# A score matmul of 64 rows takes 128, with zeros beside the keys' low parts

## The chip, the cores and the metric

The kernel runs on one core of one Trainium2 chip. The metric is the device time of one launch in microseconds. Of the core's engines five matter: PE multiplies matrices (its loads of weights are shown as PEld), DVE does elementwise work and reductions, ACT applies functions and copies, POOL does some elementwise work, and SP issues most transfers. They run side by side, each in its own program order, and wait for each other by semaphores.

## The reference, cut to what matters

One layer of a decoder trunk: 1024 tokens of 1024 channels, everything in float32. A combined projection feeds four mixers, one of which is a differential attention; gates, an output projection, a SwiGLU network and a gated embedding follow. The attention, with the other parts left out:

```python
q = q.reshape(b, s, ATT_HEADS, ATT_V_DIM)          # 4 heads of 128 = 2 x 64
k = k.reshape(b, s, ATT_HEADS, ATT_V_DIM)
k1, k2 = k[..., :ATT_QK_DIM], k[..., ATT_QK_DIM:]
...
def softmax_map(qh, kh):
    sc = jnp.einsum("bqhd,bkhd->bhqk", qh, kh).astype(jnp.float32) * scale + bias
    sc = jnp.where(causal, sc, NEG_LOGIT)
    return jax.nn.softmax(sc, axis=-1)

probs = softmax_map(qblk[..., :ATT_QK_DIM], k1) - lam * softmax_map(qblk[..., ATT_QK_DIM:], k2)
return jnp.einsum("bhqk,bkhd->bqhd", probs.astype(v.dtype), v)
```

Each head has two score maps, each over 64 channels of queries and keys. Queries are taken in blocks of 128; a block sees the keys up to its own end.

## The kernel before, in words

To keep float32 accuracy, each operand of a matmul is split into a high part (rounded to float32r) and a low part (what is missing). A product is then three matmuls: high by high, low by high, high by low (`mm3`, lines 160 to 166). The high part is an ACT copy, the low part a DVE subtraction, or for some weights a POOL subtraction (`split`, lines 72 to 74).

The program starts with the norm of x, its transposes, the values of two heads and the queries and keys of head 0. From about 100 us it runs the attention (`attention`, line 395): four heads of eight query blocks in one stream. Per block PE computes the scores of the *next* block (`scores`), transposes the probabilities of this one (`turn`), does a piece of other projections that no head depends on (the `fills`: the queries and keys of the following head, the values of heads 2 and 3, and in the last head the projections of the conformer branch, whose convolution taps run on DVE), and multiplies by the values (`weigh`). Between a block's scores and its transposes lie, on DVE and ACT, the bias, the row maximum, the exponential of each map and the difference of the two maps.

A score map has 64 channels, half of PE's 128 rows. The queries of a map are therefore held as high parts above low parts (`qs[m]`, 128 rows), and the keys' high parts twice (`kh[m]`, 128 rows), so that one matmul of 128 rows gives high by high plus low by high (line 303). The third product, high queries by low keys, is a matmul over the map's own 64 rows (line 304): the low parts of both maps share one tile `kl[0]`, map 0 in rows 0 to 63 and map 1 in rows 64 to 127, and the queries' high parts lie in the same rows. Map 1 has the halves swapped for that. Both matmuls add into one score tile in PSUM. A score tile is at most 512 columns wide per matmul, so a block of up to 512 keys has two such pairs (one per map), a wider one four.

Each engine runs what is written in program order, as far as its data allow. The tiles `qs`, `kh`, `kl` come from a pool `up` of 38 buffers of 4 KB per partition (line 46), which the later stages use as well. The low parts of the weights of the `fills` are computed on POOL (`eng=nc.gpsimd`, line 771), in order of their use.

After the attention come gates and branch projections, the other mixers, the output projection, the SwiGLU network and the gated embedding, all of them long runs of `mm3`.

Of the kernel before, what the change touches and what calls it, by code (L numbers as in the profile page):

```python
# [11 lines left out]
F32 = mybir.dt.float32  # L12
# [26 lines left out]
def tile_hybrid_layer(ctx: ExitStack, tc: tile.TileContext, a):  # L39
# [35 lines left out]

# [1 line left out]
    ident = cpool.tile([P, P], F32, name="ident")  # L77
# [24 lines left out]
    class HalfT:  # L102
        """A channel-major activation [1024 channels, 1024 tokens] as hi and lo parts."""

# [14 lines left out]
    def transpose_in(pool, tag, src, dst, t):  # L119
        """Eight 128-blocks of src [tokens of tile t, 1024] into dst, split."""  # L120
        h, c0 = t // 4, (t % 4) * P
        for b in range(2):
            ps = pool.tile([P, HF], F32, tag=tag, name=nm("tr"))
            for j in range(4):
                k = 4 * b + j
                nc.tensor.transpose(ps[:, j * P:(j + 1) * P], src[:, k * P:(k + 1) * P], ident)
            v = ps.rearrange("p (g j c) -> p g j c", g=2, j=2)
            for g in range(2):
                hi = dst.hi[h][2 * b + g][:, :, c0:c0 + P]
                lo = dst.lo[h][2 * b + g][:, :, c0:c0 + P]  # L130
                split(hi, lo, v[:, g])

    def load_w(src, nk=NK, eng=None):
        """A column tile [nk * 128, 128] of a weight as hi and lo."""
        raw = wp.tile([P, NK, P], F32, tag="raw", name=nm("raw"), bufs=RAW_BUFS)
        nc.sync.dma_start(raw[:, :nk, :], src.rearrange("(k p) c -> p k c", p=P))
        hi = wp.tile([P, NK, P], F32R, tag="whi", name=nm("whi"))
        lo = wp.tile([P, NK, P], F32R, tag="wlo", name=nm("wlo"))
        split(hi[:, :nk, :], lo[:, :nk, :], raw[:, :nk, :], eng)
        return hi, lo  # L140

    def load_row_w(src, shape, eng=None):
        """As load_row, in the slots of the column tiles."""
        raw = wp.tile(shape, F32, tag="raw", name=nm("raw"), bufs=RAW_BUFS)
        nc.sync.dma_start(raw, src)
        hi = wp.tile(shape, F32R, tag="whi", name=nm("whi"))
        lo = wp.tile(shape, F32R, tag="wlo", name=nm("wlo"))
        split(hi, lo, raw, eng)
        return hi, lo

    def load_row(src, shape, eng=None):
        """Rows of a weight as moving operands: hi and lo in slots of their own."""
        raw = wp.tile(shape, F32, tag="raw", name=nm("raw"), bufs=RAW_BUFS)
        nc.sync.dma_start(raw, src)
        hi = utile(shape, F32R, "rwh")
        lo = utile(shape, F32R, "rwl")
        split(hi, lo, raw, eng)
        return hi, lo

    def mm3(ps, triples, start=True, stop=True):  # L160
        """Sum of exact products of split operands: hi*hi + hi*lo + lo*hi."""
        n = len(triples)
        for i, (lh, ll, rh, rl) in enumerate(triples):
            nc.tensor.matmul(ps, lhsT=lh, rhs=rh, start=start and i == 0, stop=False)  # L164
            nc.tensor.matmul(ps, lhsT=lh, rhs=rl, start=False, stop=False)  # L165
            nc.tensor.matmul(ps, lhsT=ll, rhs=rh, start=False, stop=stop and i == n - 1)  # L166
# [15 lines left out]

# [1 line left out]
    ed = dram.tile([S, D], F32, name="ed")  # L184
# [37 lines left out]
    def load_v(b, load, eng=None):  # L222
        """The value columns of heads 2b and 2b+1, as moving operands."""
        c = C_V + b * 256
        return [load(w_in[q * 512:(q + 1) * 512, c:c + 256].rearrange("(k p) c -> p k c", p=P), [P, 4, 256], eng)
                for q in range(2)]

    def proj_v(b, t, wv):
        """Values of token tile t, per head the hi part beside the lo part."""
        if t % 2 == 0:  # L230
            v_hl[b, t // 2] = utile([P, 2, 2, 2, P], F32R, "vhl")
        ps = mmtile("pv")
        mm3(ps[:, 0:256], [(hT.his(k, t * P, P), hT.los(k, t * P, P), wv[k // 4][0][:, k % 4, :],
                            wv[k // 4][1][:, k % 4, :]) for k in range(NK)])
        v = v_hl[b, t // 2][:, t % 2]
        split(v[:, :, 0, :], v[:, :, 1, :], ps[:, 0:256].rearrange("p (h c) -> p h c", c=P))

    def proj(col, evac, eng=None):
        """Columns col..col+127 of the input projection, channel-major, to evac(half, psum): two steps."""
        w = []  # L240

        ps = {}

        def step(h, part):
            if not w:
                w.extend(load_w(w_in[:, col:col + P], eng=eng))
            hi, lo = w
            if part == 0:
                ps[h] = mmtile("pz")
            ks = range(part * 4, part * 4 + 4)  # L250
            mm3(ps[h], [(hi[:, k, :], lo[:, k, :], hT.his(k, h * HF, HF), hT.los(k, h * HF, HF)) for k in ks],
                part == 0, part == 1)
            if part == 1:
                evac(h, ps[h])

        return [lambda h=h, part=part: step(h, part) for h in range(2) for part in range(2)]

# [1 line left out]
    def proj_qk(h, eng=None):  # L259
        """Of both score maps: queries as hi above lo, keys as hi above hi, and the keys' lo parts; the  # L260
        products over 128 rows are then hi*hi + lo*hi in one pass. Map 1 has the halves swapped."""
        qs, kh, kl = [None] * 2, [None] * 2, [None]
        own = (slice(0, 64), slice(64, P))
# [10 lines left out]
        def evac_k(half, ps):  # L274
            s = slice(half * HF, (half + 1) * HF)
            for m in range(2):
                if half == 0:
                    kh[m] = utile([P, S], F32R, "kh")
                    if m == 1:
                        kl[0] = utile([P, S], F32R, "kl")  # L280
            for m in range(2):
                r, o = own[m], own[1 - m]
                nc.scalar.activation(kh[m][r, s], ps[r], AF.Copy)
                nc.scalar.activation(kh[m][o, s], ps[r], AF.Copy)
                nc.vector.tensor_sub(kl[0][r, s], ps[r], kh[m][r, s].bitcast(F32))

        return (qs, kh, kl), proj(C_Q + h * P, evac_q, eng) + proj(C_K + h * P, evac_k, eng)

    def head(h, qk):
        """One head: its steps per query block and the step that ends it."""  # L290
        q_st, k_hi, k_lo = qk
# [4 lines left out]
        def scores(i):  # L296
# [4 lines left out]
            def score(ps, m, c0, c1):  # L301
                r = slice(m * 64, (m + 1) * 64)
                nc.tensor.matmul(ps, lhsT=q_st[m][:, qs], rhs=k_hi[m][:, c0:c1], start=True, stop=False)
                nc.tensor.matmul(ps, lhsT=q_st[m][r, qs], rhs=k_lo[0][r, c0:c1], start=False, stop=True)

# [89 lines left out]
    def attention(qk, fills):  # L395
        """All heads as one stream of query blocks; the steps of `fills`, which a head does not depend on, lie
        between its blocks."""
        heads, y, ended = {}, [], 0
# [21 lines left out]

# [1 line left out]
    merged = [None] * NK  # L422
# [31 lines left out]

# [1 line left out]
    def conv(c, src, name, bias, j, K, t0, n, ops=None):  # L456
        """c = causal depthwise convolution of src, for tokens t0..t0+n-1 of channel tile j, as single steps."""
        def tap(k):
# [69 lines left out]

# [1 line left out]
    def lru():  # L530
# [58 lines left out]

# [1 line left out]
    def sconv(ys):  # L591
# [57 lines left out]

# [1 line left out]
    hT = HalfT("hT")  # L651
# [22 lines left out]

    # relative-position bias of the two key blocks next to a query block, times 8, less the far bucket's
    tdf = stile(4, "tdf")
# [16 lines left out]

    # per-channel vectors, channels on partitions
    vecs = [("lru_conv_w", 4), ("lru_conv_b", 1), ("lru_ba", 1), ("lru_bx", 1), ("lru_lambda", 1),
# [27 lines left out]

    # lambda of the differential attention, negated, on every partition
    lv = t2tile("lv")
# [10 lines left out]

    # 8 * softplus(-lru_lambda) = 8 * (max(z, 0) + log1p(exp(-|z|))), log1p(e) = 2 atanh(e / (2 + e))
    lam4 = cvec[:, :, pos["lru_lambda"]]
# [28 lines left out]

# [1 line left out]
    fills = []  # L769
# [51 lines left out]

# [1 line left out]
    wo = [load_row(a["w_o"][0][k * P:(k + 1) * P, :], [P, D]) for k in range(NK)]  # L823
# [31 lines left out]

# [1 line left out]
    acc = [None] * NT  # L857
# [68 lines left out]

# [1 line left out]
    out = a["out"][0]  # L928
# [39 lines left out]
def bucket_hot():  # L968
    """Column j is the one-hot T5 bucket of distance 255 - j; zero where the distance is negative."""
    n = 255 - np.arange(384)  # L970
# [24 lines left out]
```

## Time and profile before

| | |
|---|---|
| median of 3 timed runs | 2092.32 us (2092.0 to 2092.96) |
| span of the profiled execution | 2090.1 us |
| PE busy | 2058.9 us (99%), 9405 matmuls |
| DVE busy | 1045.2 us (50%) |
| ACT busy | 696.4 us (33%) |
| POOL busy | 46.5 us (2%), 25 instructions |
| chain that ended last | PE 90%, DVE 5%, DMA 3%, ACT 2% |

The profiled execution's own time, its span, is 2.2 us under the median; the page gives no other time for it. In the profile an engine counts as busy from an instruction's start to its end. PE works on several matmuls at once, one behind the other, so the rows of matmuls that follow each other overlap, and the distance between two starts tells more than a duration. A row of a timeline has the start, the duration, the engine, the line, the operation, what it writes and reads by the program's names, and the shape; "64*128" of a matmul are the rows and columns of its weights, "64x512" the shape of what streams past them. A bracket at a row's end is the time that the engine idled before it, and what it waited for.

### The profile page before, as it was taken

The numbers are of one execution on the slowest core, as the hardware profiler recorded it, in microseconds if no ns is written. First come the engines' busy times: TensorE is split into PE (matmuls) and PEld (weight loads), VectorE is DVE, ScalarE is ACT, GpSimd is POOL, SyncE is SP. The second block draws the span as 40 slices with busy tenths as digits, with TensorE's granted clock in tenths as the row PEclk, the third lists the DMA queues.
The fourth block names the chain that finished last, engine by engine and source line by source line (L and its number), as shares of the span: only waits on it lengthen the run. The fifth ranks groups of instructions, "written<-read, shape, count | busy, mean of one in ns | idle before, by whom it ended". The sixth has DMA issues, their size and how long they took to land.

```text
span 2090.1 us, 22768 instructions
## 1 busy us (share of the span) xinstructions
PE 2058.9 (99%) x9405; PEld 1685.8 (81%) x9405; DVE 1045.2 (50%) x1507; ACT 696.4 (33%) x1167; POOL 46.5 (2%) x25
## 2 busy tenths in 40 slices
PE   7999999999999999999999999999999999999999
PEld 6867877888887888878888788888888888888787
DVE  4476669697957323464333544233434333343574
ACT  5455555422115212563222433321111211112374
POOL 1000111000000000000000000000000000000000
PEclk9999999999999999999999999999999999999999
DMA  7210110011210112112111521211202212022342
GB/s 239 74 31 21 31 31 28 23 46 46 61 51 26 56 50 58 44 31 65 46 51 46 161 101 61 61 61 41 60 21 61 61 41 61 21 61 61 101 136 96
DMA packets 155974, 126.55 MB, mean 61 GB/s; under 512 B 5616, under 2 KB 140721, under 8 KB 155870
## 3 DMA queue, kind: packets, MB, share of 16 engines
q1 hardware_dynamic: 150688, 116.93, 18.2%
q10 hardware_dynamic: 5182, 8.16, 1.1%
q8 instruction: 74, 1.21, 0.2%
q14 instruction: 30, 0.25, 0.0%
HBM read 111.70 MB, written 13.37 MB: 60 GB/s over the span
## 4 chain that ended last, share of the span: by engine, by line
PE 90%; DVE 5%; DMA 3%; ACT 2%; issue 1%; ACTq 0%; DVEq 0%; SPq 0%
PE pz L164 5%; PE pz L165 5%; PE pz L166 5%; PE pg L166 5%; PE pg L165 5%; PE pg L164 5%; PE fu L165 4%; PE fu L166 4%; PE fg L165 4%; PE fg L166 4%; PE fu L164 4%; PE fg L164 4%; PE fo L166 4%; PE fo L164 4%; PE fo L165 4%; PE pb L166 3%
## 5 line engine op out<-in xcount | busy, mean ns | idle before, releaser
L74 DVE TENSOR_TENSOR wlo<-raw,whi 128x1024 fp32r<-128x1024 f32 (+1 forms) x130 | 141.8, 1091 | 339.5 <-ACT whi L73 339.3
L73 ACT ACTIVATE whi<-raw 128x1024 fp32r<-128x1024 f32 (+1 forms) x148 | 143.4, 969 | 462.3 <-PE pg L165 123.4
L164 PE MATMUL pz<-hTh,whi 128*128 128x512 f32 x576 | 229.5, 398 | 2.0 <-ACT scc L600 1.7
L166 PE MATMUL pz<-hTh,wlo 128*128 128x512 f32 x576 | 227.2, 394 | 0.0
L165 PE MATMUL pz<-hTl,whi 128*128 128x512 f32 x576 | 227.1, 394 | 0.0
L166 PE MATMUL pg<-hTh,wlo 128*128 128x512 f32 x512 | 199.1, 389 | 0.5 <-DVE wlo L74 0.5
L165 PE MATMUL pg<-hTl,whi 128*128 128x512 f32 x512 | 199.3, 389 | 0.0
L164 PE MATMUL pg<-hTh,whi 128*128 128x512 f32 x512 | 199.2, 389 | 0.0
L464 DVE SCALAR_TENSOR_TENSOR cfc<-cfu,cvec,cfc 128x994 f32<-128x994 f32 (+14 forms) x120 | 160.4, 1337 | 2.6
L875 DVE TENSOR_TENSOR fsilu<-fu,fsilu 128x512 f32<-128x512 f32 x44 | 30.4, 692 | 259.5 <-PE fu L166 259.5
L893 DVE TENSOR_TENSOR acc<-acc,fo 128x512 f32<-128x512 f32 x160 | 108.9, 686 | 80.8 <-PE fo L166 79.5
L164 PE MATMUL fo<-rwh,fh 128*128 128x512 f32 x352 | 137.5, 390 | 0.2
L165 PE MATMUL fo<-rwl,fh 128*128 128x512 f32 x352 | 137.2, 390 | 0.0
L166 PE MATMUL fu<-h2Th,wlo 128*128 128x512 f32 x352 | 137.0, 389 | 0.0
L166 PE MATMUL fo<-rwh,fl 128*128 128x512 f32 x352 | 137.0, 389 | 0.0
L165 PE MATMUL fu<-h2Tl,whi 128*128 128x512 f32 x352 | 136.9, 389 | 0.0
L164 PE MATMUL fu<-h2Th,whi 128*128 128x512 f32 x352 | 136.9, 389 | 0.0
L164 PE MATMUL fg<-h2Th,whi 128*128 128x512 f32 x352 | 136.9, 389 | 0.0
L165 PE MATMUL fg<-h2Tl,whi 128*128 128x512 f32 x352 | 136.9, 389 | 0.0
L166 PE MATMUL fg<-h2Th,wlo 128*128 128x512 f32 x352 | 136.9, 389 | 0.0
L164 PEld LDWEIGHTS pz<-hTh,whi 128*128 128x128 f32 x576 | 109.0, 189 | 26.9 <-issue 2.8
L166 PEld LDWEIGHTS pz<-hTh,wlo 128*128 128x128 f32 x576 | 108.7, 189 | 24.0 <-issue 1.9
(265 smaller groups left out, 3809.8 us busy)
## 6 DMA issues: line engine op xcount, KB each, us to landing
raw<-in_w_in_dram SPq DMA_DIRECT2D x72, 512.0 KB, 3.8
raw<-in_w_ffn_in_dram SPq DMA_DIRECT2D x44, 512.0 KB, 4.1
raw<-in_w_ffn_out_dram SPq DMA_DIRECT2D x22, 512.0 KB, 3.5
raw<-in_w_branch_dram SPq DMA_DIRECT2D x32, 256.0 KB, 2.7
xt<-in_x_dram SPq DMA_DIRECT2D x8, 512.0 KB, 5.4
ed<-e ACTq DMA_DIRECT2D x16, 256.0 KB, 2.7
xres<-in_x_dram SPq DMA_DIRECT2D x8, 512.0 KB, 4.1
raw<-in_w_o_dram SPq DMA_DIRECT2D x8, 512.0 KB, 5.3
```

The lines of the kernel that those rows point to most:

```text
L73: nc.scalar.activation(dst_hi, src, AF.Copy)
L74: (eng or nc.vector).tensor_sub(dst_lo, src, dst_hi.bitcast(F32))
L164: nc.tensor.matmul(ps, lhsT=lh, rhs=rh, start=start and i == 0, stop=False)
L165: nc.tensor.matmul(ps, lhsT=lh, rhs=rl, start=False, stop=False)
L166: nc.tensor.matmul(ps, lhsT=ll, rhs=rh, start=False, stop=stop and i == n - 1)
L464: nc.vector.scalar_tensor_tensor(o, in0=src[:, a0 - sh:t0 + n - sh], scalar=cv(name, j, k), in1=o, op0=ALU.mult, op1=ALU.add)
L875: nc.vector.tensor_mul(g, pu, g)
L893: nc.vector.tensor_add(acc[t][:, cs], acc[t][:, cs], ps)
```

## The change

The keys' low parts get a tile per map, `kl[0]` and `kl[1]`. Each holds the low parts in the map's own 64 rows, and zeros in the other 64, which POOL writes once per head. Line 304 then multiplies all 128 rows: the queries' low parts meet the zeros.

```diff
-        qs, kh, kl = [None] * 2, [None] * 2, [None]
+        qs, kh, kl = [None] * 2, [None] * 2, [None] * 2
...
                     kh[m] = utile([P, S], F32R, "kh")
-                    if m == 1:
-                        kl[0] = utile([P, S], F32R, "kl")
+                    kl[m] = utile([P, S], F32R, "kl")
+                    nc.gpsimd.memset(kl[m][own[1 - m], :].bitcast(F32), 0.0)
...
-                nc.vector.tensor_sub(kl[0][r, s], ps[r], kh[m][r, s].bitcast(F32))
+                nc.vector.tensor_sub(kl[m][r, s], ps[r], kh[m][r, s].bitcast(F32))
...
             def score(ps, m, c0, c1):
-                r = slice(m * 64, (m + 1) * 64)
                 nc.tensor.matmul(ps, lhsT=q_st[m][:, qs], rhs=k_hi[m][:, c0:c1], start=True, stop=False)
-                nc.tensor.matmul(ps, lhsT=q_st[m][r, qs], rhs=k_lo[0][r, c0:c1], start=False, stop=True)
+                nc.tensor.matmul(ps, lhsT=q_st[m][:, qs], rhs=k_lo[m][:, c0:c1], start=False, stop=True)
```

The rest of the diff drops comments. On PE, DVE, ACT and SP the same instructions stand in the same order; names carry other numbers. On PE these are the scores of the first two blocks of head 0, two maps each (`sc` is the score tile, `kh` and `kl` the keys' parts, `qs` the queries). Before:

```order
L303 MATMUL sc_1029<-kh_726,qs_689 128x128
L304 MATMUL sc_1029<-kl_728,qs_689 128x128
L303 MATMUL sc_1029<-kh_727,qs_692 128x128
L304 MATMUL sc_1029<-kl_728,qs_692 128x128
L303 MATMUL sc_1048<-kh_726,qs_689 128x256
L304 MATMUL sc_1048<-kl_728,qs_689 128x256
```

And now:

```order
L303 MATMUL sc_1032<-kh_726,qs_689 128x128
L304 MATMUL sc_1032<-kl_727,qs_689 128x128
L303 MATMUL sc_1032<-kh_729,qs_692 128x128
L304 MATMUL sc_1032<-kl_730,qs_692 128x128
L303 MATMUL sc_1051<-kh_726,qs_689 128x256
L304 MATMUL sc_1051<-kl_727,qs_689 128x256
```

Nothing moved; the second map reads a low tile of its own. On POOL the memsets come in. From the low parts of the embedding's weights (`wlo_110`) to those of head 1's queries and keys and of the next weights, before:

```order
L74 TENSOR_TENSOR wlo_110<-raw_107,whi_109 128x1024
L74 TENSOR_TENSOR wlo_1075<-raw_1072,whi_1074 128x1024
L74 TENSOR_TENSOR wlo_1315<-raw_1312,whi_1314 128x1024
L74 TENSOR_TENSOR wlo_1611<-raw_1608,whi_1610 128x1024
L74 TENSOR_TENSOR wlo_1770<-raw_1767,whi_1769 128x1024
```

And now:

```order
L74 TENSOR_TENSOR wlo_110<-raw_107,whi_109 128x1024
L281 MEMSET kl_727 64x1024
L281 MEMSET kl_730 64x1024
L74 TENSOR_TENSOR wlo_1078<-raw_1075,whi_1077 128x1024
L74 TENSOR_TENSOR wlo_1318<-raw_1315,whi_1317 128x1024
L281 MEMSET kl_1406 64x1024
L281 MEMSET kl_1409 64x1024
L74 TENSOR_TENSOR wlo_1617<-raw_1614,whi_1616 128x1024
L74 TENSOR_TENSOR wlo_1776<-raw_1773,whi_1775 128x1024
```

A pair of memsets per head stands in front of a subtraction. The same further on, at the two halves of the value weights of heads 2 and 3 and the weights that follow; before:

```order
L74 TENSOR_TENSOR wlo_1889<-raw_1886,whi_1888 128x1024
L74 TENSOR_TENSOR wlo_1895<-raw_1892,whi_1894 128x1024
L74 TENSOR_TENSOR wlo_2402<-raw_2399,whi_2401 128x1024
L74 TENSOR_TENSOR wlo_2561<-raw_2558,whi_2560 128x1024
L74 TENSOR_TENSOR wlo_2680<-raw_2677,whi_2679 128x1024
```

And now:

```order
L74 TENSOR_TENSOR wlo_1898<-raw_1895,whi_1897 128x1024
L281 MEMSET kl_1805 64x1024
L281 MEMSET kl_1808 64x1024
L74 TENSOR_TENSOR wlo_1904<-raw_1901,whi_1903 128x1024
L74 TENSOR_TENSOR wlo_2411<-raw_2408,whi_2410 128x1024
L74 TENSOR_TENSOR wlo_2570<-raw_2567,whi_2569 128x1024
L281 MEMSET kl_2599 64x1024
L281 MEMSET kl_2602 64x1024
L74 TENSOR_TENSOR wlo_2692<-raw_2689,whi_2691 128x1024
```

Head 2's pair stands between the two halves of the value weights, head 3's behind the second weights of the projections that follow.

## Rows read from the trace of the kernel before

**Rows 1.** Windows: busy us (and count) of PE, PEld, DVE, ACT, POOL; clock, DMA.

```profile
173.30:245.00 71.70, 70.20 (x428) 58.10 (x428) 46.56 (x97) 38.34 (x92) 9.50 (x4) 1.00 0.10 30
245.00:307.00 62.00, 62.00 (x292) 47.59 (x290) 35.62 (x74) 36.99 (x74) 7.69 (x4) 1.00 0.09 26
307.00:402.00 95.00, 93.12 (x430) 72.71 (x429) 82.26 (x124) 47.09 (x97) 13.40 (x5) 0.96 0.11 31
307.00:350.00 43.00, 41.12 (x184) 32.14 (x182) 38.94 (x59) 20.86 (x48) 7.06 (x3) 0.92 0.11 31
```

**Rows 2.** Timeline of PE in an input projection of head 2: start us, duration us.

```profile
300.07 0.40 PE L165 MATMUL pz<-hTl,whi 128*128 128x512 f32 x1
300.30 0.40 PE L166 MATMUL pz<-hTh,wlo 128*128 128x512 f32 x1
```

**Rows 3.** Timeline of PE in scores of head 0 and of head 1.

```profile
100.86 0.33 PE L303 MATMUL sc<-kh,qs 128*128 128x128 f32 x1
101.11 0.32 PE L304 MATMUL sc<-kl,qs 64*128 64x128 f32 x1
101.37 0.38 PE L303 MATMUL sc<-kh,qs 128*128 128x256 f32 x1
101.68 0.38 PE L304 MATMUL sc<-kl,qs 64*128 64x256 f32 x1
102.00 0.38 PE L303 MATMUL sc<-kh,qs 128*128 128x256 f32 x1
...
208.90 0.49 PE L303 MATMUL sc<-kh,qs 128*128 128x512 f32 x1
209.32 0.50 PE L304 MATMUL sc<-kl,qs 64*128 64x512 f32 x1
209.75 0.33 PE L352 MATMUL ptr<-ident,prob 128*128 128x128 f32 x1
```

**Rows 4.** Source line 304: durations min/median/max in ns, first and last start, forms.

```profile
L304 PE MATMUL sc<-kl,qs x96: 322/490/580, 100.6 to 389.1; 64*128 64x512 f32 x48, 64*128 64x128 f32 x16, 64*128 64x256 f32 x16, 64*128 64x384 f32 x16
```

**Rows 5.** Timeline of PE: 128-row neighbours of 128 and of 256 columns.

```profile
180.99 1.06 PE L389 MATMUL otr<-ident,oall 128*128 128x128 f32 x8 [1.50 <-DVE mx L324]
181.81 0.48 PE L165 MATMUL pz<-hTl,whi 128*128 128x512 f32 x1
...
216.22 0.28 PE L363 MATMUL av<-vhl,pth 128*128 128x256 f32 x1
216.34 0.28 PE L364 MATMUL av<-vhl,ptl 128*128 128x256 f32 x1
```

**Rows 6.** Timeline of PE's weight loads in the projection of rows 2.

```profile
299.84 0.19 PEld L165 LDWEIGHTS pz<-hTl,whi 128*128 128x128 f32 x1
```

**Rows 7.** Timeline of POOL, PE and DVE: results and the matmuls that read them.

```profile
194.73 2.39 POOL L74 TENSOR_TENSOR wlo<-raw,whi 128x1024 fp32r<-128x1024 f32 x1 [17.22 <-ACT whi L73]
197.18 0.39 PE L165 MATMUL pv<-wlo,hTh 128*128 128x256 f32 x1
...
215.10 1.14 DVE L342 SCALAR_TENSOR_TENSOR prob<-prob,ratio,prob 128x896 f32<-128x896 f32 x1
220.97 0.98 PE L352 MATMUL ptr<-ident,prob 128*128 128x128 f32 x7
```

**Rows 8.** Timeline of PE and DVE: where PE waits in head 0 and head 3.

```profile
110.64 0.44 PE L303 MATMUL sc<-kh,qs 128*128 128x384 f32 x1 [0.24 <-ACT prob L312]
122.32 0.44 PE L352 MATMUL ptr<-ident,prob 128*128 128x128 f32 x1 [1.96 <-DVE prob L342]
307.10 3.23 DVE L464 SCALAR_TENSOR_TENSOR cfc<-cfu,cvec,cfc 128x994 f32<-128x994 f32 x1
310.57 1.11 PE L352 MATMUL ptr<-ident,prob 128*128 128x128 f32 x4 [1.58 <-DVE oall L369]
```

**Rows 9.** Groups of instructions on POOL: busy us, mean ns, idle before.

```profile
L532 POOL MEMSET bd<- 128x1024 f32 x1 | 1.0, 960 | 424.8 <-PE pb L166 424.8
```

**Rows 10.** Windows, columns as in rows 1.

```profile
310.00:315.00 5.00, 4.43 (x12) 3.47 (x13) 5.00 (x11) 2.29 (x8) 0.00 (x0) 0.50 0.36 107
```

## The prediction, made before the changed kernel was run

> **What bounds the kernel now.** I first read the windows view of the attention, the stage in which the change lies [rows 1]. In each stretch PE is the busy engine (70.2 of 71.7 us, 62.0 of 62.0, 93.1 of 95.0), and DVE comes near it only in the last head (82.3 of 95.0). But a PE that counts as busy need not be streaming: a matmul's row lasts until its result is out, so I read starts, not durations. In the timeline of an input projection, 512-column matmuls over 128 rows, each with new weights, start 0.23 us apart [rows 2]. In the timeline of the scores the same width is far slower: line 303 (128 rows) at 208.90, line 304 (64 rows) at 209.32, the next 128-row instruction at 209.75 [rows 3]. That is 0.42 and 0.43 us, about the whole duration of one matmul: wherever the row count changes, the next one starts only when the one before is through. Line 303 has the full shape and is hit as hard as line 304, so it isn't the small matmul that is slow, but the step from 128 to 64 rows and the step back. It happens at every width: 0.25 and 0.26 us at 128 columns (100.86, 101.11, 101.37), 0.31 and 0.32 us at 256 (101.37, 101.68, 102.00) [rows 3].
>
> **The change part by part.** *The second matmul takes 128 rows.* All neighbours then have one shape, and the starts should fall to what 128-row neighbours show: 0.23 us at 512 columns [rows 2], 0.12 at 256 (216.22 to 216.34), and about 0.10 at 128 (eight transposes of 128 columns between 180.99 and 181.81) [rows 5]. For a pair of lines 303 and 304 that saves 0.85 - 0.46 = 0.39 us at 512 columns, 0.63 - 0.24 = 0.39 at 256 and 0.51 - 0.21 = 0.30 at 128. 384 columns lie between two widths that save 0.39, and I take that. The source view counts 48 pairs of 512 columns and 16 each of 384, 256 and 128 [rows 4]: 80 x 0.39 + 16 x 0.30 = 36.0 us, or 9.0 per head. The bound above is that sum, since line 304 can't be cheaper than the neighbours that it comes to equal. The bound below is no gain at all, if the gap belonged to something else in the pair (that both matmuls carry the same queries as weights and add into one bank). Lines 164 to 166 add into one bank as well, with 0.23 us between starts [rows 2], so I take the upper end.
>
> A rule of the skill speaks against this. The Trainium skill, "TensorE: Matmul & The Clock Gate", section "Part 3: Packing small matmuls", says that a weight load overlaps a running matmul only when the row groups differ; with full rows everywhere each load would stand behind the matmul before it. The trace disagrees: with 128 rows on both sides the load of line 165 runs at 299.84 for 0.19 us, and the matmuls around it stay 0.23 us apart [rows 2, 6].
>
> *What comes back as waits.* PE's order is the same before and after, so each saved piece brings PE earlier to results of DVE, ACT and POOL. In most blocks there is room: the probabilities that DVE finishes at 216.24 (215.10 + 1.14) are transposed at 220.97, 4.7 us later, and a block of eight matmuls takes out at most 4 x 0.39 = 1.6 us [rows 7]. There is none in three places:
> - The first four blocks of head 0. The scores of blocks 0 and 1 are issued early, and the third block at 110.64 already waits for an exponential; what blocks 0 and 1 save (2 x 0.30 + 2 x 0.39 = 1.4 us) returns whole. At 122.32 PE has waited 1.96 us for probabilities [rows 8], so of the 1.6 us of blocks 2 and 3 I let 1.3 return, as only their own scores shorten that chain. Together 2.7 us.
> - Head 3, where DVE works off the convolution's taps between the softmax steps. PE waits 1.58 us there at 310.57, behind a tap of 3.23 us [rows 8]. DVE's highest share in a stretch is 38.94 / 43.0 = 0.91 [rows 1]. If it can't pass that, the 95.0 us shrink to 82.26 / 0.91 = 90.8, so 4.2 of the 9.0 us stay and 4.8 return.
> - Edges in heads 1 and 2 where PE starts right behind a result that the scores don't bring forward: POOL's low parts end at 197.12 (194.73 + 2.39) and line 165 starts at 197.18 [rows 7]; the end of a head has PE waiting 1.50 us at 180.99 [rows 5]. About 1 us at each of three such edges, an estimate from these rows, 3.1 us in all.
>
> That returns 10.6 us, and 36.0 - 10.6 = 25.4 stay.
>
> *Eight memsets on POOL.* Each head clears half of two tiles. The only memset of 1024 columns in the trace takes 0.96 us [rows 9], so a pair is 1.9 us and all are 7.7. POOL is the least busy engine (13.4 of 95.0 us at most [rows 1]), and the pairs run when the subtraction before them is done, long before the scores that read them. In front of the next subtraction POOL has idled 17.22 us at 194.73 [rows 7], which covers a pair; if that cover went, a pair would cost up to 1.9 us at one edge. What they may cost beside that is DVE's time, where the two engines hold each other up. Bounds: nothing, or all 7.7 us. I take nothing, since POOL's busy time is far from the length of any stretch and the first pair, by its place in POOL's order, falls well before the attention; the pair between the two halves of the value weights lies nearest to a wait of PE for DVE (180.99 [rows 5]). Here the Trainium skill, "SBUF - State Buffer", section "Who interferes with whom", says that a DVE instruction with two SBUF inputs contends with a GpSimd instruction that reads SBUF, not with one that only writes; by it the price is nothing too, and no run here shows it yet.
>
> *One more 4 KB tile per head* from the 38-buffer pool. It could make later tiles wait. In the built program PE, ACT, DVE and SP wait for the same instructions as before, apart from three waits of DVE for memsets that are long done by then. So nothing.
>
> *The clock.* It is at 1.2 instead of 2.4 GHz in stretches such as 310 to 315 us (mean 0.50), after PE had idled 1.58 us [rows 8, 10]. A longer wait there may lengthen that, by 1 or 2 us, and a removed one may save as much. I count zero and keep it in the range.
>
> The sum: the profiled execution spans 2090.1 us, the timed runs have 2092.3, so some 2.2 us lie around the span and stay. 2090.1 - 25.4 = 2064.7, and 2092.3 - 25.4 = **2067 us** for the timed runs.
>
> **The rivals.**
> 1. *All of it is kept* (2092.3 - 36 = 2056 us): the chains follow PE. For it, the 4.7 us of room in the middle of a head; against it, the waits that stand in rows 8 before anything is saved. A gain over 32 us counts here.
> 2. *The softmax chain takes most.* If heads 1 and 2 keep no more than head 3 (4.2 us each) and head 0 loses its 2.7 us on top: 4 x 4.2 - 2.7 = 14 us, 2078 us. Against it, DVE is busy only 46.6 of 71.7 and 35.6 of 62.0 us there [rows 1]. A gain between 6 and 18 us counts here.
> 3. *The gap stays*, since each weight load (0.19 us [rows 6]) has to follow the matmul before it: a pair of 512 columns then takes 2 x (0.19 + 0.23) = 0.84 us instead of 0.85, and the time stays at about 2092 us. This is the rule cited above. Against it, rows 2 and 6. The change would then not do what it says.
> 4. *Slower: POOL.* Each pair of memsets stands in front of a subtraction on whose result the next projection's matmuls wait, and may hold DVE as well. Up to 25.4 / 4 = 6.3 us per pair that only eats the gain; beyond it the kernel is slower. With 8 us per pair, 2092.3 - 25.4 + 32 = 2099 us. Against it, a pair is 1.9 us long, a third of what it would take.
>
> **How the numbers follow.** Forecast (gain 18 to 32 us) 0.68; rival 1 0.14; rival 2 0.13; rival 3 0.03; rival 4 0.02. The likeliest case alone spans 2060 to 2074. The range goes to the whole 36 us below (2056, with one more for the clock) and to rival 2 above with some 3 us for clock and memsets: 2055 to 2081. A measurement here can tell 0.2%, 4.2 us, from no change. Faster: 0.68 + 0.14 + 0.13 = 0.95; same 0.03; slower 0.02.
>
> **What would show it.** The starts of lines 303 and 304 (304 in the new numbering too) 0.23 us apart at 512 columns and 0.12 at 256: step one right; 0.4 as before: wrong, and rival 3 holds. PE's waits in the attention growing by about 11 us, most of it at the start of head 0 and in head 3, behind DVE and ACT (now 1.96 and 1.58 us at the two largest places [rows 8]): step two right; if they grow by less than 4 us, rival 1; by more than 18, rival 2. The new MEMSET rows on POOL, with a DVE instruction beside them that takes its usual time: the memsets' price of nothing right. The work that now ends at 402 us should end near 377, and all behind it only shift. I am wrong in kind if a wait appears behind the attention, or if a low clock fills more of the attention than before.

## The result, and the profile after

The changed kernel takes 2065.72 us (median of 4 runs, 2062.73 to 2067.35) against 2092.64 us of the kernel before beside it, 26.9 us less. The ratio on record is 0.9863 [0.9848, 0.9879]; it is not the quotient of these two medians (0.9871), and of 2092.64 us it would be 28.7 us (25.3 to 31.8). The forecast was 2067. The profiled execution spans 2062.6 us, 27.5 less than before.

The difference lies almost wholly in the attention. Set side by side, PE's starts stand 0.4 us later than before when the attention begins and 26.9 us earlier from 375 us on (402 before), so the attention is 27.3 us shorter. They stay there until 1966 us (1993 before), where 0.6 us more come from a shorter wait for ACT (0.2 us in place of 0.8). In the windows view PE is busy 1672.73 us behind the attention, and was 1672.63.

PE in the scores of one block of head 1, timeline of the kernel before (start us, duration us, engine, line); this run of scores is longer than that of [rows 3]:

```profile
217.54 0.28 PE L364 MATMUL av<-vhl,ptl 128*128 128x256 f32 x1
217.66 0.39 PE L303 MATMUL sc<-kh,qs 128*128 128x512 f32 x1
217.98 0.49 PE L304 MATMUL sc<-kl,qs 64*128 64x512 f32 x1
218.40 0.50 PE L303 MATMUL sc<-kh,qs 128*128 128x512 f32 x1
218.83 0.50 PE L304 MATMUL sc<-kl,qs 64*128 64x512 f32 x1
...
220.97 0.98 PE L352 MATMUL ptr<-ident,prob 128*128 128x128 f32 x7
```

The same block after, and two maps of 256 columns of head 0, the counterparts of the second half of [rows 3]'s first group:

```profile
101.43 0.28 PE L304 MATMUL sc<-kl,qs 128*128 128x256 f32 x1
101.55 0.28 PE L303 MATMUL sc<-kh,qs 128*128 128x256 f32 x1
101.66 0.28 PE L304 MATMUL sc<-kl,qs 128*128 128x256 f32 x1
...
203.52 0.28 PE L364 MATMUL av<-vhl,ptl 128*128 128x256 f32 x1
203.64 0.40 PE L303 MATMUL sc<-kh,qs 128*128 128x512 f32 x1
203.87 0.40 PE L304 MATMUL sc<-kl,qs 128*128 128x512 f32 x1
204.11 0.39 PE L303 MATMUL sc<-kh,qs 128*128 128x512 f32 x1
204.34 0.40 PE L304 MATMUL sc<-kl,qs 128*128 128x512 f32 x1
...
205.49 0.71 PE L352 MATMUL ptr<-ident,prob 128*128 128x128 f32 x5
```

In these rows the starts are now 0.23 to 0.24 us apart at 512 columns and 0.11 to 0.12 at 256. The four pairs took 220.97 - 217.66 = 3.31 us and take 1.85. Note the first pair of before: from 303 to 304 it lost only 0.1 us (0.32 apart), from then on each start lost 0.2 (0.42 and 0.43).

The price is in PE's waits in the attention: who waited, for whom, us in total, times, longest. (`ptr` are the transposes of the probabilities, `prob` the probabilities; `oall` are a head's output rows, which DVE adds up out of the PSUM buffers that `ptr` shares with the products `av`; `wlo` and `ptl` are low parts of weights and of probabilities.)

```profile
PE ptr L352 <- DVE oall L369: 5.4, 3, 2.3
PE sc L303 <- ACT prob L312: 3.7, 3, 1.7
PE pv L165 <- POOL wlo L74: 1.2, 1, 1.2
PE av L363 <- DVE ptl L74: 1.0, 1, 1.0
PE ptr L352 <- DVE prob L342: 0.5, 1, 0.5
```

With two waits of 0.4 and 0.3 us that makes 12.5 us, where the kernel before has 6.1: 2.0 and 1.5 for the two single waits of [rows 8] and [rows 5], 1.9 for oall in head 3, and 0.7 in small ones. So 6.4 us came back. The two heaviest waits of head 3 read like this after, in the timeline of all engines:

```profile
283.45 2.79 POOL L74 TENSOR_TENSOR wlo<-raw,whi 128x1024 fp32r<-128x1024 f32 x1 [12.67 <-ACT whi L73]
284.06 3.23 DVE L464 SCALAR_TENSOR_TENSOR cfc<-cfu,cvec,cfc 128x994 f32<-128x994 f32 x1
287.21 0.27 DVE L369 TENSOR_TENSOR oall<-oall,av 128x128 f32<-128x128 f32 x1
287.55 1.12 PE L352 MATMUL ptr<-ident,prob 128*128 128x128 f32 x4 [2.33 <-DVE oall L369]
...
334.10 2.38 POOL L74 TENSOR_TENSOR wlo<-raw,whi 128x1024 fp32r<-128x1024 f32 x1 [11.70 <-PE av L364]
337.47 0.27 DVE L369 TENSOR_TENSOR oall<-oall,av 128x128 f32<-128x128 f32 x1
337.80 0.33 PE L352 MATMUL ptr<-ident,prob 128*128 128x128 f32 x1 [1.91 <-DVE oall L369]
```

A tap (line 464) takes 1.26 us at the median and 3.23 where POOL computes weights' low parts at the same time; the output row behind it is late, and PE waits. What follows such a wait stands in the windows view (columns as in [rows 1]):

```profile
287.40:290.40 3.00, 2.85 (x10) 2.57 (x11) 3.00 (x7) 1.86 (x7) 0.00 (x0) 0.50 0.58 175
338.70:341.70 3.00, 3.00 (x8) 2.33 (x8) 3.00 (x6) 2.41 (x4) 0.00 (x0) 0.50 0.28 85
```

The granted clock is 0.50 (1.2 GHz) there, for 3.4 us each time. Before, the attention had 3.4 us of this at 123 us and 6.8 us at 310 us [rows 10]; after it has 6.8 in all, so the clock gave 1.7 us back.

### The profile page after: what moved, and what is told of

It is laid out like the page before. It is cut to its first block, busy times and chain, and to the rows that moved or that the text cites. A ratio compares the mean times of both kernels' runs of the same rounds, so it can differ in the third digit from the quotient of the medians.

```text
span 2062.6 us, 22787 instructions
## 1 busy us (share of the span) xinstructions
PE 2025.4 (98%) x9405; PEld 1680.2 (81%) x9405; DVE 1043.2 (51%) x1507; ACT 696.3 (34%) x1167; POOL 53.7 (3%) x33
## 4 chain that ended last, share of the span: by engine, by line
PE 83%; DVE 6%; ACT 2%; DMA 1%; issue 1%; POOL 0%; ACTq 0%; POOLq 0%; DVEq 0%
PE pg L166 5%; PE pg L165 5%; PE pg L164 5%; PE pz L164 4%; PE pz L165 4%; PE pz L166 4%; PE fu L166 4%; PE fu L165 4%; PE fu L164 4%; PE fg L164 4%; PE fg L165 4%; PE fg L166 4%; PE fo L166 4%; PE fo L165 4%; PE fo L164 4%; PE pb L166 3%
## 5 line engine op out<-in xcount | busy, mean ns | idle before, releaser
L872 ACT ACTIVATE fsilu<-fg 128x512 f32<-128x512 f32 x44 | 26.1, 594 | 304.2 <-PE fg L166 304.1
```

Source lines behind the costliest of these rows:

```text
L872: nc.scalar.activation(g, pg, AF.Silu)
```

## The experiments

Each was compared with runs of the kernel before on the same chip.

**Two halves of the change apart.** First the order alone: the kernel before with both 128-row matmuls of a pair of maps first and then both 64-row ones, so that the row count changes half as often.

```diff
-            def score(ps, m, c0, c1):
-                r = slice(m * 64, (m + 1) * 64)
-                nc.tensor.matmul(ps, lhsT=q_st[m][:, qs], rhs=k_hi[m][:, c0:c1], start=True, stop=False)
-                nc.tensor.matmul(ps, lhsT=q_st[m][r, qs], rhs=k_lo[0][r, c0:c1], start=False, stop=True)
+            def score(parts):
+                for ps, m, c0, c1 in parts:
+                    nc.tensor.matmul(ps, lhsT=q_st[m][:, qs], rhs=k_hi[m][:, c0:c1], start=True, stop=False)
+                for ps, m, c0, c1 in parts:
+                    r = slice(m * 64, (m + 1) * 64)
+                    nc.tensor.matmul(ps, lhsT=q_st[m][r, qs], rhs=k_lo[0][r, c0:c1], start=False, stop=True)
```

> The kernel before (64-row second matmul, no zeros), with the two pairs that stand side by side regrouped: both 128-row matmuls first, then both 64-row ones. Theory (each change of the row count makes the next matmul wait for the one before to be through): the changes are halved. Two 128-row matmuls and two 64-row ones of 512 columns in a row start 0.23 us apart each, the two steps between the kinds stay near 0.32 to 0.43; about half of the 30 us of gaps that the changed kernel removed go, 13 to 16 us, a third of it comes back as waits: 2077 to 2084 us. Rival (the 64-row matmul is slow by itself, whatever stands beside it): the two 64-row matmuls still start 0.43 us apart, and only the gap after the first 128-row one goes, 5 to 9 us: 2084 to 2088 us.

Measured: 2078.43 us (2077.19 to 2081.13), ratio 0.9922 [0.9907, 0.9937]. Summed from the start of each score matmul to the next start, 69.7 us of the kernel before became 52.3, where the change brings them to 42.0: 17.5 of 27.7 us, over half. PE's timeline of this kernel, first a group of head 0 whose two 64-row matmuls lie in different row halves (`x2` is two in one row), then two 128-row and two 64-row matmuls of one row half, with 384 and 512 columns (306 is its 64-row line):

```profile
103.19 0.33 PE L306 MATMUL sc<-kl,qs 64*128 64x128 f32 x2
...
203.54 0.39 PE L306 MATMUL sc<-kl,qs 64*128 64x512 f32 x1
203.86 0.44 PE L303 MATMUL sc<-kh,qs 128*128 128x384 f32 x1
204.14 0.40 PE L303 MATMUL sc<-kh,qs 128*128 128x512 f32 x1
204.46 0.44 PE L306 MATMUL sc<-kl,qs 64*128 64x384 f32 x1
204.74 0.39 PE L306 MATMUL sc<-kl,qs 64*128 64x512 f32 x1
205.07 0.33 PE L352 MATMUL ptr<-ident,prob 128*128 128x128 f32 x1
```

From 203.86 on starts are 0.28, 0.32, 0.28 and 0.33 us apart, where 0.18 and 0.23 would be streaming: each of the four is 0.10 too long, though only two of them change the row count (the 303 of 203.86 itself stands behind a 64-row matmul). So a change costs 0.1 us at the start that follows it and 0.1 at the next one. Where every matmul changes the count the two add up to the 0.2 of before. The rival, that a 64-row matmul is slow by itself, falls: then 303 to 303 would lose nothing and 306 to 306 0.2. What I expected between two matmuls of one kind, 0.23 us at 512 columns, was wrong too. "Mode switching requires drain", says the Trainium skill, TensorEngine Tiling (Array Packing), section "Key Properties". The trace agrees that the change of shape is what costs, at 0.10 us for each of two starts; that the engine drains it does not show, since by the profile's ends the matmul of 204.14 still runs (0.40 us) when the next one starts 0.32 us behind it.

Not all of the 17.5 us come from fewer changes. In 16 of the 48 groups (the blocks of up to 512 keys) the two 64-row matmuls lie in different row halves, and they start 3 ns apart: both stand in the 0.33 us of 103.19. Two of the same half start 0.16 to 0.34 us apart, by width, so running side by side is worth about 4.0 us, an estimate from these distances. The other 13.5 us are half of what the change gains, as half the changes should be.

Then the tiles and the memsets alone, with the matmul still over 64 rows:

```diff
-                nc.tensor.matmul(ps, lhsT=q_st[m][:, qs], rhs=k_lo[m][:, c0:c1], start=False, stop=True)
+                nc.tensor.matmul(ps, lhsT=q_st[m][r, qs], rhs=k_lo[m][r, c0:c1], start=False, stop=True)
```

> The changed kernel's tiles and memsets (a low tile per map, zeros beside), but the second matmul over the map's own 64 rows as before. Theory: the gain is all in the row count, the tiles and memsets cost and bring nothing: 2091 to 2094 us, gaps of 0.42 and 0.43 us as before. Rival (part of the change's gain comes from the two tiles, each map reading its own): 2070 to 2088 us. Rival (the memsets cost what POOL takes for them): 2094 to 2100 us.

Measured: 2093.2 us (2091.05 to 2097.62), ratio 0.9993 [0.9984, 1.0003]. Eight memsets and four more tiles cost nothing that can be told; the whole gain is the row count's.

Last, the changed kernel in the order of the first experiment (both matmuls with `k_hi`, then both with `k_lo[m]`, all 128 rows):

```diff
+                for ps, m, c0, c1 in parts:
+                    nc.tensor.matmul(ps, lhsT=q_st[m][:, qs], rhs=k_lo[m][:, c0:c1], start=False, stop=True)
```

> The changed kernel (128 rows everywhere) with the same regrouping as in the first kernel. Theory: there is no row change left, so the order of the four is worth nothing: within 3 us of the changed kernel's 2066. Rival (what counts is that the two matmuls of a pair add into one score tile one right after the other, or use the same weights): a further 5 us or more are gained.

Measured: 2067.86 us (2066.67 to 2068.58), ratio 0.9868 [0.9852, 0.9884], the changed kernel's own time. Where all shapes are alike the order is worth nothing.

**The memsets' price.** The changed kernel with each memset written three times:

```diff
-                    nc.gpsimd.memset(kl[m][own[1 - m], :].bitcast(F32), 0.0)
+                    for _ in range(3):
+                        nc.gpsimd.memset(kl[m][own[1 - m], :].bitcast(F32), 0.0)
```

> The changed kernel with each memset written three times: 24 of 0.95 us on POOL instead of 8. Theory: they lie where POOL idles and cost PE nothing: within 3 us of the changed kernel's 2066. Rival (the memsets are on the path of the low parts of weights, or hold DVE up): the 15 us more of POOL's time cost 5 to 15 us: 2071 to 2081.

Measured: 2070.72 us (2069.7 to 2072.78), ratio 0.9885 [0.987, 0.99]. That is 4.7 us above 2066, a miss of the theory's 3 us, and just under the rival's 2071; the regrouped kernel on the same chip takes 2.9 us less. Beside the changed kernel's trace 2.4 us arise in the start-up, at a wait that ends 2.2 us later in the changed kernel's second trace too (below). Then 1.4 us come at 112 to 117 us, behind head 1's memsets: PE waits 2.32 us for an exponential where it waited 1.70, and a stretch at 1.2 GHz follows. Another 1.4 come at 125 to 130 us with a second such stretch of 3.4 us, which a trace of the changed kernel without the extra memsets shows as well. None come at the tripled memsets of heads 2 and 3; 3 us more come far behind the attention. The timeline of POOL and DVE at head 1's, the densest place:

```profile
104.83 4.00 POOL L282 MEMSET kl<- 64x1024 f32 x4
105.91 0.16 DVE L757 TENSOR_TENSOR ser<-ser,at 128x4 f32<-128x4 f32 x1
106.11 0.74 DVE L758 TENSOR_SCALAR ser<-ser 128x4 f32<-128x4 f32 x1
106.89 0.16 DVE L757 TENSOR_TENSOR ser<-ser,at 128x4 f32<-128x4 f32 x1
107.08 0.77 DVE L758 TENSOR_SCALAR ser<-ser 128x4 f32<-128x4 f32 x1
...
109.08 0.17 DVE L758 TENSOR_SCALAR ser<-ser 128x4 f32<-128x4 f32 x1
```

A memset holds up DVE's one-input TENSOR_SCALAR (0.77 us in place of 0.17) until it ends, and leaves the TENSOR_TENSOR with two inputs alone. Four such rows lose some 2 us of DVE here, an estimate from these durations; that this lengthens the wait for the exponential is likely, but not shown. So memsets written three times are not free, and a part goes through DVE, as the rival said. With single memsets that befalls two tiny rows (0.75 and 0.65 us at 100.66), too little to see in the time of the tiles alone.

**The waits that came back.** Three attempts to move DVE's work out of their way. The changed kernel again, as a base on that chip:

> The changed kernel once more, to stand beside the next three on the same chip: 2064 to 2069 us, PE's waits in the attention 12 to 13 us.

2067.74 us (2063.48 to 2069.86), ratio 0.987 [0.9854, 0.9887], with the same waits to 0.1 us. Its starts stand 2.2 us later than in the first profile from 33 us on, before the attention begins; this start-up difference, 0 to 3.4 us from trace to trace, makes most of what the profiled executions of the changed kernel differ by (3.0 to 3.3 us).

Fewer taps between the softmax steps of head 3:

```diff
-        conv_some(1)
+        conv_some(i % 2)
...
-    gates(0, split_all(y_att), first=True, between=lambda n: conv_some(4))
+    gates(0, split_all(y_att), first=True, between=lambda n: conv_some(5))
```

> The changed kernel with one convolution tap at every other step of head 3 instead of at each (12 taps, some 15 us of DVE, move behind the attention, where five taps lie beside a gate instead of four). Theory (what head 3 gives back it gives back because DVE can't keep up there): PE's waits of about 6 us behind DVE in head 3 shrink to about 2, the time falls by 3 to 5 us below the changed kernel. Rival (the waits there are the softmax chain's own length, not DVE's load): the same within 1.5 us. Rival (the taps come back as waits behind the attention): the same or slower.

2067.62 us (2066.28 to 2069.99), ratio 0.9873 [0.9859, 0.9888]: a miss. The waits are the same (oall 5.4 us), and the tap of 3.23 us still stands in front of the first of them. The number of taps was not what PE waits for.

The bias block of attention's start computed earlier, within the norm's loop (18 lines moved up under `if t == 4:`):

```diff
+        if t == 4:
+            tdf = stile(4, "tdf")
...
-    tdf = stile(4, "tdf")
```

> The changed kernel with the bias table's matmuls and its two transfers written before the queries of head 0 (at the fifth token tile) instead of after. Theory (the first blocks of head 0 give their saving back since their softmax waits for the bias transfer): the first bias add comes some 4 us earlier, PE's 3.7 us of waits for the exponential shrink to under 1, the time falls by 2 to 4 us below the changed kernel. Rival (the chain of the first blocks is bound by ACT and DVE, or the early transfer holds ACT's queue up in the start): the same within 1.5 us, or slower by up to 5.

2066.59 us (2065.08 to 2069.45), ratio 0.9869 [0.9854, 0.9884], and with both edits:

> Both edits in one kernel, the candidate for a better version. Theory: the two add up, 5 to 9 us below the changed kernel: 2057 to 2061 us where that has 2066. Rival: neither brings anything, 2064 to 2068.

2067.69 us (2065.39 to 2069.15), ratio 0.9873 [0.9857, 0.989]. Two more misses. By the trace the bias's work costs PE 2 to 3 us where it now stands (64 to 106 us) and gives 4 us back in head 0 (sc waits 2.2 in place of 3.7 us). In the first of the two a stretch at 1.2 GHz at 185 us takes 1.8 us back, in the second 1.1 us of start-up differ; what is left can't be told from nothing.

Then the other reading of the timeline: not the taps are too many, but POOL makes them long. The eight weight splits of the last projections go from POOL to DVE (the expectations from here on write VectorE for DVE and GpSimd for POOL).

```diff
-            return proj(C_CG + j * P, evac_g, nc.gpsimd) + proj(C_CA + j * P, evac_a, nc.gpsimd)
+            return proj(C_CG + j * P, evac_g) + proj(C_CA + j * P, evac_a)
```

> The changed kernel with the eight weight splits of the last projections inside the attention (cf_proj, line 492) on VectorE in place of GpSimd. Theory: the waits of PE behind VectorE in head 3 (three of oall, 5.4 us together) come from GpSimd's splits of 2.39 us, during which a tap of VectorE takes 2.6 to 3.4 us in place of 1.27 (five of the rows of line 464 do). With the splits on VectorE (about 1.3 us each by the rows of 128x1024) these long taps are gone, the waits for oall shrink to under 2 us, and the time is 2 to 4 us under that of the changed kernel beside it (about 2062 to 2064). Rival: VectorE is simply full in head 3 (0.91 of the stretch), eight splits of 1.3 us cost it as much as the five long taps did, and the waits stay within 1 us of 5.4: the time is the same within 1 us. Other sign: a split queued in VectorE's order ahead of a softmax row delays it by 1.3 us each time, 8 times, or the projection waits for its split: 2068 to 2075.

> The changed kernel again, beside the two others on this chip: 2065 to 2068 us and three waits for oall of 5.4 us together; both theories.

Measured: 2059.21 us (2056.69 to 2061.11), ratio 0.9838 [0.9823, 0.9852], beside 2068.16 us (2065.8 to 2069.6), ratio 0.9881 [0.9865, 0.9898], of the changed kernel on that chip. PE's waits with the splits on DVE:

```profile
PE sc L303 <- ACT prob L312: 3.2, 3, 1.6
PE pv L165 <- POOL wlo L74: 1.2, 1, 1.2
PE av L363 <- DVE ptl L74: 1.0, 1, 1.0
PE av L364 <- DVE ptl L74: 0.4, 1, 0.4
PE ptr L352 <- DVE oall L369: 0.3, 1, 0.3
PE pz L164 <- DVE qs L273: 0.3, 1, 0.3
```

The taps, grouped (durations min/median/max in ns), in the changed kernel:

```profile
L464 DVE SCALAR_TENSOR_TENSOR cfc<-cfu,cvec,cfc x30: 1207/1264/3367, 284.1 to 357.5; 128x994 f32<-128x994 f32 x1, 128x995 f32<-128x995 f32 x1, 128x996 f32<-128x996 f32 x1, 128x997 f32<-128x997 f32 x1
```

and with the splits on DVE:

```profile
L464 DVE SCALAR_TENSOR_TENSOR cfc<-cfu,cvec,cfc x30: 1212/1264/1283, 286.9 to 361.6; 128x994 f32<-128x994 f32 x1, 128x995 f32<-128x995 f32 x1, 128x996 f32<-128x996 f32 x1, 128x997 f32<-128x997 f32 x1
```

The windows of this kernel that hold the places of the two low stretches:

```profile
284.00:300.00 16.00, 15.69 (x95) 13.76 (x94) 15.66 (x31) 8.83 (x24) 0.00 (x0) 1.00 0.12 34
326.00:345.00 19.00, 19.00 (x102) 16.32 (x101) 18.66 (x27) 7.63 (x18) 0.00 (x0) 1.00 0.10 28
```

No tap is longer than 1.28 us, the waits in head 3 fell from 5.9 to 0.3 us, and the clock stays at 2.4 GHz there (a low stretch of 3.4 us at 124 us, in head 0, remains). Between 259 and 345 us this kernel gains 9.2 us on the first profile of the changed one: 5.6 of waits and 2 x 1.7 of clock make 9.0. On the profile from its own chip, where the same waits were followed by one low stretch only, it gains 7.8 there, and 2.6 more of the spans' difference is start-up. I had expected 2 to 4, since I had counted the waits in part and the clock behind them not at all. DVE pays eight splits of 1.22 us for it, and has the room: it is busy 18.66 of 19.00 us from 326 us on without PE waiting for it. This agrees with the Trainium skill, SBUF — State Buffer, section Who interferes with whom, by which a DVE instruction with two SBUF inputs contends with a GpSimd instruction that reads SBUF; here each of the five long taps of the changed kernel ends 1.05 to 1.08 us behind the POOL subtraction beside it, so the tap stands still until POOL is nearly through.

The same for the queries' and keys' splits of heads 1 to 3 as well:

```diff
-        qk[h], f = proj_qk(h, nc.gpsimd)
+        qk[h], f = proj_qk(h)
```

> As e9, and also the splits of the projections of queries and keys of heads 1 to 3 on VectorE (line 771). Theory: GpSimd's rows in heads 0 to 2 hold VectorE too, but there no wait of PE for VectorE was above 1 us, so nothing more is gained: within 1 us of e9. Rival (VectorE full): six more splits of 1.3 us in heads 0 to 2, where the softmax of the first blocks is waited for: 2 to 4 us longer than e9.

2063.25 us (2061.21 to 2064.37), ratio 0.9857 [0.9842, 0.9871]: 4 us above the last one, as the rival had it. A wait for a maximum appears at the end of head 0 (177 us), and the clock is at 1.2 GHz for 3.4 us behind it:

```profile
PE otr L389 <- DVE mx L324: 2.3, 1, 2.3
```

In this kernel POOL is the wrong place for a split where DVE has room, and the right one where DVE's next row is waited for.

The kernel before with the splits of head 3 on DVE:

> The kernel before (64-row second score matmul) with the eight splits of cf_proj on VectorE in place of GpSimd. Theory: the kernel before lost less to GpSimd's splits than the changed one: its waits for oall (1.9 us) and the one of otr for mx (1.5 us) stand at 310 us beside a tap of 3.23 us, and the 6.8 us at 1.2 GHz follow them (3.4 us lost). Without them it gains 5 to 7 us, 2086.5 to 2088.5 where the kernel before has 2093.6. Then the changed kernel and this one with the same splits stand 28 to 31 us apart, which is the saving of the gaps alone (30.3 by the two traces). Rival: the clock falls for another reason and stays low for 6.8 us: it gains 2 to 3.5 us only, 2090 to 2091.5. Other sign: VectorE's extra 8 x 1.2 us come on the path here, since PE waited little before: 2094 or more.

2090.8 us (2088.24 to 2093.68), ratio 0.998 [0.9971, 0.9989]. PE's waits in its attention:

```profile
PE ptr L352 <- DVE prob L342: 2.0, 1, 2.0
PE otr L389 <- DVE mx L324: 1.5, 1, 1.5
PE pz L164 <- DVE qs L272: 0.3, 1, 0.3
PE sc L303 <- ACT prob L312: 0.2, 1, 0.2
```

The waits for oall (1.9 us) are gone and with them the 6.8 us at 1.2 GHz of [rows 10]: 1.9 + 3.4 = 5.3, and its attention is 5.2 us shorter by the traces. (The 1.5 us for mx, which I had put there, belong to the end of head 0 [rows 5] and stay.) The time alone does not decide: 4.2 us under the kernel before on that chip (2094.99 us) lie between the theory's 5 to 7 and the rival's 2 to 3.5; that the low clock went with the waits, which the rival denied, decides for the theory. So before this interference cost 4 to 5 us, after the change 9. With the splits of head 3 on DVE in both kernels the change is worth 0.9838 / 0.998 = 0.9858, 29.7 us (26 to 33 by the two intervals), and 30.2 us in the attention's traces.

## Why the prediction was right

The step that carried it held: the gap belongs to the change of row count, not to the small matmul, the shared queries or the bank. How the gap arises I had wrong: the next matmul does not wait until the one before is through, since at 217.98 it starts 0.32 us behind a row of 0.39. A change costs 0.10 us at each of two starts, and what looked like a whole duration was two changes falling on one start. Most of the signs came: 0.23 and 0.12 us between starts, little but a shift behind the attention, no more low clock than before. Two did not: the waits grew by 6.4 us where I had said about 11, and rows of DVE beside the memsets were held up. Rival 3, with its rule on weight loads, is out. The gain lies between the bounds set for rivals 1 and 2 (18 and 32 us), and so does the growth of the waits (4 and 18 us). Point by point:

- **The gaps, forecast 36.0 us.** The gaps beside line 304 fell from 69.5 to 40.6 us. With 1.3 us of new waits in them put back that is 30.2 us saved, and 29.8 without the stretches of low clock. The mis-sized term is the saving per pair. I took it from pairs in the middle of a run of scores [rows 3], 0.39 us. But 43 of the 96 pairs stand behind another 128-row matmul, as that of 217.66, and lost 0.1 us less: 43 x 0.11 = 4.7, and 36.0 - 4.7 = 31.3. Of this the five starts with a wait or a low clock, left out of the 29.8, take about 1.0, an estimate at 0.2 each. 3.0 us more lie past the runs, at the second start behind each, which I had not counted, and 0.9 were lost at other starts: 31.9 in all.
- **The waits, forecast 10.6 us.** 6.4 returned. Head 3: 4.0 for 4.8, behind DVE as said, but not because DVE is full: POOL holds its taps. The share of 0.91 that I took for DVE's ceiling is none, as DVE reaches 0.98 (18.66 of 19.00 us) with the splits on it; that the number came close is luck. The edges of heads 1 and 2: 0.7 for 3.1; the wait of 1.50 us at the end of head 0 [rows 5], which I had counted there, is gone, and two of 1.2 and 1.0 came. Head 0: 1.7 for 2.7; the wait of 1.96 us of [rows 8] disappeared, and 3.3 us more for exponentials came, about half of it ahead of that place and half behind.
- **The two errors offset**, which is luck: 36.0 stood for 31.9 and 10.6 for 6.4, 4.1 and 4.2 us too large. 31.9 - 6.4 + 1.7 of clock = 27.2, against 25.4 forecast and 27.3 in the attention's traces.
- **The memsets at nothing**: right in the sum (the tiles and memsets alone: 0.9993 [0.9984, 1.0003]), though two tiny rows of DVE beside them did not keep their usual time (0.75 and 0.65 us for 0.17 and 0.15). **The pool's tiles**: right, by the tiles alone. **The clock at zero**: 1.7 us in the profile; the changed kernel's three profiles (6.8, 3.4 and 6.8 us at 1.2 GHz in the attention) differ by as much.

What stays open is why the start-up differs by up to 3.4 us before 33 us; no run was aimed at it. The traces show where it arises. PE waits 3.48 us for an ACT copy (line 211) in the first trace of the changed kernel and 6.64 in the second, and ACT stands there behind a weight split whose transfer lets it begin at 25.63 us in one and 27.90 in the other. In or behind that wait the clock is at 1.2 GHz for 3.4 us in the first, 6.8 in the second and 10.2 in the third. Open too is what in the engine makes a change of row count cost two starts.

## What to carry to other kernels

Read the distance between starts, not durations, and look for where the row count of neighbouring matmuls changes: filling a 64-row matmul between 128-row ones up to 128 rows with zeros cost no streaming time here (0.23 us between starts at 512 columns) and saved 0.2 to 0.4 us per pair. Take the saving from a whole run, its first and last members included, not from its middle. Where PE waits behind a DVE instruction that is longer than its like, look at what POOL does beside it before moving DVE's work: the version with both, at 2059.21 us, is the fastest found.

## What the hardware showed that I had not expected

- A change of row count is paid twice, 0.10 us at each of the next two starts (at 256 columns and more).
- Two 64-row matmuls of different halves start 3 ns apart in the regrouped kernel (103.191 and 103.194 us) and run beside each other; two of the same half are 0.28 us apart at 384 columns first, where 128-row ones have 0.18; the 0.10 is the second start behind the change of row count.
- A POOL subtraction of 2.4 us stretches a DVE tap from 1.26 to as much as 3.37 us, while a POOL memset leaves instructions with two inputs at 0.16 us and stretches one-input TENSOR_SCALAR rows from 0.17 to 0.77.
- The clock fell to 1.2 GHz for 3.4 us behind the wait of 1.91 us in head 3 in all three profiles of the changed kernel, which nearly doubles the wait's price, but behind the one of 2.33 us in one of the three only. With the bias block earlier it was the other way round: 3.4 us behind the wait of 2.32, none behind the one of 1.91.
